# A hybrid decoder trunk on one core: more down-projection fetches and weight sums moved forward, one block of sums taken out of the up weights' buffers, merge operands without precedence

## The chip, the cores and the metric

The kernel runs on one core of a Trainium2 chip. The metric is device time in microseconds (us). The engines are TensorE (PE, with its weight loads as PEld), VectorE (DVE), ScalarE (ACT), GpSimd (POOL) and SyncE (SP), which issues all DMAs here, one after the other in a fixed order.

## The reference

One layer of a decoder trunk on x of 1024 tokens by 1024 features, float32. The two mixers, which the change does not touch, are left out here.

```python
h = rms_norm(x, norm_mix_pre);  proj = h @ w_in          # columns for mixers A, B and two gates
y_a = gdn_branch(...) @ w_out_a                          # gated DeltaNet, 4 heads
y_b = gla_branch(...) @ w_out_b                          # gated linear attention, 4 heads
merged = sigmoid(gate_a) * y_a + sigmoid(gate_b) * y_b
x = x + rms_norm(merged @ w_o, norm_mix_post)            # called x1 below
h = rms_norm(x, norm_mlp_pre)
u = square(relu(h @ w_mlp_up))                           # 1024 x 4096
x = x + rms_norm(u @ w_mlp_down, norm_mlp_post)
```

## The kernel before

**Arithmetic.** Every float32 operand is cut into a high part (rounded to the PE's fp32r type by a cast on ACT) and a low part (the rest, a subtraction on DVE, in fp32r as well). A 128x512 output over 128 of the contraction takes three matmuls (high by high, high by low, low by high). `split` and `hilo` do the cutting; in the listings a weight `w` becomes `wh` and `wl`, and a `big` or `R` tile holds both parts of a block. A "product" is a 128x128x4 block of weights against a 512x512 block of activations: four steps of three, twelve matmuls (L68).

**Stages.** Input projection and mixers; the merge stage, whose `load_o` fetches the mixers' outputs slice by slice and cuts each into `hi` and `lo`; the output projection W_o, in a pool `op`; the up projection, in a pool `ml`; the down projection, in a pool `dn`. The MLP's two multiplications are done as seven products of sums of blocks instead of eight products of blocks (Strassen-Winograd): tokens and features are halved, and P1 to P7 are the seven products. A "unit" n is one pair of 128-wide column blocks of w_mlp_up (columns n and n + 16 blocks), so there are 16 units (NU). Units 0 to 7 (NE = 8) have their P1 and P2 computed ahead, in the `op` stage, and do five products in the up stage (`early`); units 8 to 15 do seven.

**The `op` stage.** For token half u = 0, then 1, W_o is multiplied in, and each of the half's four 128-token tiles goes through this chain: x is loaded into `xt` (L1194, tag "ss", two buffers); x1 is made in it on DVE (L175) and stored to DRAM, `d_x1` (L1196, `d_x` in the profile); ACT squares it (L178), POOL makes the reciprocal root (L172, L186), and DVE writes the normalised tile into `m` (L175). `turn(u, i)` then transposes tile i of half u by eight PE transposes (L72) into two PSUM banks and makes the operand blocks from them: X["11"], X["21"] and R["11"], R["21"] for u = 0; for u = 1 R["22"], and from sums with the first half's blocks T1, T2, X["22"], X["21"], by way of X["12"] (T3 and T4 follow from X["22"] and X["21"]). The four turns of u = 0 stand in the loop of the second half's W_o. Those of u = 1 stand in the loop that computes P1 and P2 of units 0 to 7, two units at a time: P1 of both, then P2 of both, so the loop has 32 products, here numbered from 0. `TURNS[1]` = (2, 4, 6, 8) puts the four turns, called turn 0 to 3 below, after the matmuls of products 2, 4, 6 and 8 of that numbering as the program is written; where the scheduler then puts them is shown further down. Of the 32 products the text below deals with the first sixteen. For each product 256 KB of weights are loaded (L1210) into a tile `raw` of the pool `wraw` (tag "w", four buffers) and cut into `wh` and `wl` (pool `wsp`, three buffers); the result is evacuated to `e` and stored to `d_p` or `d_u[0]` (L1228).

**Weights of the up stage.** `prep(n)` loads a unit's two column blocks (1 MB, as two `wu` DMAs, L1108) into a `ztile` (tag "wu", four buffers) and makes the sums for its products on DVE: three operations, and a fourth for units below 8. The four X blocks are such ztiles too, so unit 0's prep, which stands after the loop, gets the buffer of an X block. In the up stage prep(n + 2) is called in unit n.

**The down stage.** `down_sums(j)` loads three 256 KB blocks of w_mlp_down (`us`, L1304; tag "us", six buffers, which the unit's own sums, `u_sums`, share), makes two sums and stores them to `d_t`. It is called for two j in each of units 8 to 15. The down stage's seven products (in the order P1, P2, P6, P5, P7, P4, P3) read their operands by `fetch(p, j, pool, place)`, a load of 512 KB of activations (`ru`) and one of 512 KB of weights (`rv`, L1250); what it returns, `parts`, cuts both (L1269 on ACT, L166 on DVE) into a `big` tile (four buffers) when called. Each such pair feeds 24 matmuls. In the last unit, four fetches of P1 (j = 0, 2, 4, 6) are issued ahead of that unit's P3 into tiles R11 and R21, whose old contents (the operands of P1 and P2) are then no longer needed; three are cut there too, the fourth at the end of the unit.

**What sets the order.** A list scheduler places every instruction by when its operands and buffers come free in its own model and by the program's order; `tc.high_priority` lets the instructions in its block go ahead of others that are ready. Each engine then runs its list in that fixed order, and SP issues the DMAs in its list one by one: a DMA that has to wait for a buffer or for data holds up all DMAs behind it. Eight semaphores serve the DMAs in rotation.

Of the kernel before, what the change touches and what calls it, by code (L numbers as in the profile page):

```python
# [16 lines left out]
P = 128  # L17
# [116 lines left out]
def kernel(  # L134
# [30 lines left out]
    def tt(out, a, b, op, eng=None):  # L165
        (eng or V).tensor_tensor(out=out, in0=a, in1=b, op=op)  # L166
# [866 lines left out]
    with tc.tile_pool(name="mp", bufs=1, reuse_waits="tile") as mp:  # L1033
        def load_o(src, n, nm):
            hi = mp.tile([P, n, S], F32R, name=nm + "H")
            lo = mp.tile([P, n, S], F32R, name=nm + "L")
            for k in range(n):
                for u in range(2):
                    us = slice(u * 512, u * 512 + 512)
                    raw = mp.tile([P, 512], F32, tag="oraw", name="oraw", bufs=2)  # L1040
                    SP.dma_start(out=raw, in_=src[k, :, us])
                    with tc.high_priority(offset=HP):
                        A.copy(out=hi[:, k, us], in_=raw)
                        tt(lo[:, k, us], raw, hi[:, k, us].bitcast(F32), ALU.subtract)
            return hi, lo
        oaH, oaL = load_o(d_oa, 4, "oa")
        obH, obL = load_o(d_ob, 8, "ob")
        run(gate_groups([int(c) for c in GTAIL.split()]))
        hp.release()
        bot = tc.alloc_tile_pool(name="bot", bufs=4, side="right", reuse_waits="tile")  # L1050

        def big():
            return bot.tile([P, 8, 512], F32R, tag="big", name="big")

        mg_ = [(big(), big()) for _ in range(2)]
        for c in range(4):
            def sl(w):
                return lambda s: [w[:, 2 * s:2 * s + 2, c * 256:c * 256 + 256]]
            ya = gemm_fm(sl(woa), 4, oaH, oaL, banks=[[mbank("r"), mbank("o")], [mbank("l"), mbank("t")]] if c == 0 else None)
            ga = {}  # L1060
            for b in range(2):
                for u in range(2):
                    sg = mp.tile([P, 512], F32, tag="sa", name="sa", bufs=4)
                    SP.dma_start(out=sg, in_=d_sig[c * 2 + b, :, u * 512:u * 512 + 512])
                    with tc.high_priority(offset=HPE):
                        tt(sg, ya[b][u], sg, ALU.mult)
                    ga[b, u] = sg
            yb = gemm_fm(sl(wob), 8, obH, obL)
            for b in range(2):
                for u in range(2):  # L1070
                    us = slice(u * 512, u * 512 + 512)
                    sg = mp.tile([P, 512], F32, tag="sb", name="sb", bufs=2)
                    SP.dma_start(out=sg, in_=d_sig[8 + c * 2 + b, :, us])
                    with tc.high_priority(offset=HPE):
                        tt(sg, yb[b][u], sg, ALU.mult)
                    mg = ga[b, u]
                    with tc.high_priority(offset=HPM):
                        tt(mg, mg, sg, ALU.add)
                    A.copy(out=mg_[u][0][:, c * 2 + b, :], in_=mg)
                    tt(mg_[u][1][:, c * 2 + b, :], mg, mg_[u][0][:, c * 2 + b, :].bitcast(F32), ALU.subtract)  # L1080
# [19 lines left out]
    def ztile():  # L1100
        return z.tile([P, 2 * KT * P], F32, tag="wu", name="wu", bufs=4)
# [22 lines left out]


    with tc.tile_pool(name="op", bufs=1, reuse_waits="tile") as op:
        X = {n: ztile().rearrange("p (k c) -> p k c", c=512) for n in ("12", "11", "21", "22")}
        wpost = row_bc(norm_mix_post[0], D, "wpost", op)
        wpre2 = row_bc(norm_mlp_pre[0], D, "wpre2", op)

# [8 lines left out]
        def turn(u, i):  # L1139
            m = msu[u][i]  # L1140
            il = slice(i * P, i * P + P)
            pv = []
            for g in range(2):
                pt = gbank() if u else mbank("tl"[g])
                for k in range(4):
                    T.transpose(out=pt[:, k * P:(k + 1) * P], in_=m[:, (g * 4 + k) * P:(g * 4 + k + 1) * P],
                                identity=ident)
                pv.append(pt.rearrange("p (k c) -> p k c", c=P))
            if u == 0:
                for g, n in enumerate(("11", "21")):  # L1150
                    A.copy(out=X[n][:, :, il], in_=pv[g])
                    hilo(R[n], k4, il, X[n][:, :, il])
            else:
                x11, x21, x12, x22 = (X[n][:, :, il] for n in ("11", "21", "12", "22"))
                A.copy(out=x12, in_=pv[0])
                tt(x22, pv[1], x12, ALU.subtract)
                hilo(R["22"], k4, il, pv[1])
                tt(x12, x12, x11, ALU.subtract)
                tt(x11, x22, x11, ALU.add)
                hilo(T2, k4, il, x11)  # L1160
                hilo(T1, k4, il, x12)
                tt(x21, x21, x11, ALU.subtract)
# [40 lines left out]
        for n in range(0, NE, 2):  # L1203
            pair = range(n, n + 2)
            bank = {}
            for p, k0, blk in (("P1", 0, R["11"]), ("P2", 4, R["21"])):
                for m in pair:
                    raw = wraw.tile([P, 2, 256], F32, tag="w", name="w").rearrange("p a c -> p (a c)").rearrange(
                        "p (k c) -> p k c", c=P)
                    SP.dma_start(out=raw, in_=wup[:, k0:k0 + 4, m * P:m * P + P])  # L1210
                    hi, lo = split(raw, [P, 4, P], wsp, "w")
                    if p == "P1":
                        bank[m] = mbank("ro"[m % 2])
                    for k in range(4):
                        mm3(bank[m], hi[:, k, :], lo[:, k, :], blk[:, k, :], blk[:, 4 + k, :],
                            p == "P1" and k == 0, k == 3, p == "P2")
                    step = 2 * n + (2 if p == "P2" else 0) + m - n
                    if step in TURNS[1]:
                        turn(1, TURNS[1].index(step))
                    e = op.tile([P, 512], F32, tag="e", name="e", bufs=3)  # L1220
                    with tc.high_priority(offset=HPM):
                        if p == "P1":
                            A.copy(out=e, in_=bank[m])
                        else:
                            act(e, bank[m], AF.Relu)
                    if p == "P2":
                        act(e, e, AF.Square)
                    SP.dma_start(out=d_p[m] if p == "P1" else d_u[0][:, m, :], in_=e)  # L1228
        prep(0)
        T3, T4 = big(), big()  # L1230
        for k in range(0, 4, 2):
            hilo(T3, slice(k, k + 2), slice(0, 512), X["22"][:, k:k + 2, :])
# [42 lines left out]
    with tc.tile_pool(name="ml", bufs=1, reuse_waits="tile") as ml:  # L1275
# [93 lines left out]
        def s_P3(n):  # L1369
            x = un[n]  # L1370
            product(n, "P3", x["C"], False)
            with tc.high_priority(offset=HPM):
                tt(x["c12"], x["C"], x["c12"], ALU.add)
            relu2(x["c12"], x["c12"])
# [48 lines left out]
        for n in range(NU):  # L1423
            if n + 1 < NE:
                again(n + 1)
            if n < NE:
                early(n)
                u_sums(n)
                continue
            s_P6(n)  # L1430
            if n + 2 < NU:
                prep(n + 2)
            s_P5(n)
            s_P7(n)
            if n >= NU // 2:
                down_sums(2 * n - NU)
            if n + 1 < NU:
                s_P1(n + 1)
                s_P4(n)
                s_P2(n + 1)  # L1440
                s_P3(n)
            else:
                if n == NU - 1:

                    r = [hp2.tile([P, 8, 512], F32, tag=t, name="r" + t) for t in ("R11", "R21")]
                    places = [(r[q // 2][:, q % 2 * 4:q % 2 * 4 + 2], r[q // 2][:, q % 2 * 4 + 2:q % 2 * 4 + 4])
                              for q in range(4)]
                    ahead = [fetch("P1", 2 * q, None, places[q]) for q in range(4)]
                    ahead[:3] = [f() for f in ahead[:3]]
                s_P3(n)  # L1450
                s_P4(n)
            if n >= NU // 2:
                down_sums(2 * n - NU + 1)
            u_sums(n)
        ahead[3] = ahead[3]()
    z.release()


    with tc.tile_pool(name="dn", bufs=1, reuse_waits="tile") as dn:
# [4 lines left out]
        def products(p, banks, first, tail=False):  # L1464
            todo = []
            for j in range(0, NU, 2):
                todo.append((j, ahead.pop(0) if ahead else fetch(p, j, dn)()))
                if tail and j == NU - 4:
                    continue
                if tail and j == NU - 2:  # L1470
# [131 lines left out]
```

## Time and profile before

| what | value |
|---|---|
| median of 3 runs | 1677.91 us (1676.59 to 1677.92) |
| the profiled execution | 1680.88 us, of which its span is 1679.2 us |
| granted PE clock, mean | 0.996 |
| PE busy | 1637.6 us, 8398 matmuls |
| DVE, ACT, POOL busy | 1002.1, 785.9, 134.8 us |
| DMA | 255.56 MB, mean 152 GB/s |
| loads `wu` | 32 of 512 KB, 5.7 us each from issue to landing |
| loads `us` | 48 of 256 KB, 4.7 us |

In the views, a row of a timeline begins with the start and the duration in us, then the engine (SPq is SP's queue, where the time of a DMA's issue stands), the line, the operation, the tile written and the tile read, and how many like instructions follow each other; a bracket at the end gives how long the engine had idled before it and what ended that. A row of waits gives who waited, for whom, then the sum of us, the count and the longest. A row of windows gives, for a stretch, its length, each engine's busy time with its instructions, the granted PE clock (PEclk, 1.00 is full), and the share of the core's DMA engines that was busy, which can come out a little over 1.

### The profile page before, as it was taken

How to read it: one execution, taken by the hardware profiler on the slowest of the kernel's cores; microseconds unless marked ns; L12 is line 12 of the kernel's file. 1: busy time of each engine (PE TensorE's matmuls, PEld its weight loads, DVE VectorE, ACT ScalarE, POOL GpSimd, SP SyncE). 2: the span in 40 equal slices, each digit the busy share in tenths (PEclk: the TensorE clock that was granted, in tenths of full speed). 3: DMA queues.
4: the chain of work that ended last, by engine and by line, in shares of the span. 5: the costliest groups of instructions: out<-in, count | busy, mean ns of one | idle time of the engine just before them, and what ended most of it. 6: DMA issues, size and time to landing. Idle time of an engine off the chain costs nothing. (4 is left out here: it accounts for less than half of the span.)

```text
span 1679.2 us, 23073 instructions
## 1 busy us (share of the span) xinstructions
PE 1637.6 (98%) x8398; PEld 1357.6 (81%) x8398; DVE 1002.1 (60%) x1714; ACT 785.9 (47%) x1629; POOL 134.8 (8%) x225
## 2 busy tenths in 40 slices
PE   7999999999999999999999999999999999999998
PEld 6887778878888888888788888778888887888886
DVE  5677555872455548453444545988777655564764
ACT  5556554644544355343421235754555545443442
POOL 3010111111000000011100011200000000000021
PEclk9999999999999999999999999999999999999999
DMA  5222212221222212224633345686588798786764
GB/s 170 56 75 76 86 38 85 76 79 63 88 69 70 63 51 76 76 57 150 212 109 101 110 160 176 224 275 225 197 275 283 243 311 314 257 272 222 244 220 152
DMA packets 186720, 255.56 MB, mean 152 GB/s; under 512 B 23639, under 2 KB 104622, under 8 KB 186606
## 3 DMA queue, kind: packets, MB, share of 16 engines
q1 hardware_dynamic: 186606, 254.09, 46.9%
q8 instruction: 66, 1.08, 0.3%
q14 instruction: 48, 0.39, 0.1%
HBM read 190.05 MB, written 63.98 MB: 151 GB/s over the span
## 5 line engine op out<-in xcount | busy, mean ns | idle before, releaser
L68 PE MATMUL g<-hT,wh 128*128 128x512 f32 (+1 forms) x728 | 289.4, 398 | 3.1 <-ACT sg L178 2.3
L68 PE MATMUL g<-hL,wh 128*128 128x512 f32 (+1 forms) x728 | 283.4, 389 | 0.0
L68 PE MATMUL g<-hT,wl 128*128 128x512 f32 (+1 forms) x728 | 283.1, 389 | 0.0
L166 DVE TENSOR_TENSOR wl<-w,wh 128x512 fp32r<-128x512 f32 x197 | 135.4, 689 | 215.7 <-ACT wh L237 206.6
L237 ACT CAST wh<-w 128x512 fp32r<-128x512 f32 x200 | 123.7, 619 | 211.7 <-PE g L68 202.4
L68 PE MATMUL g<-big 128*128 128x512 f32 x768 | 175.3, 389 | 2.2 <-ACT big L1269 2.2
L68 PEld LDWEIGHTS g<-big 128*128 128x128 f32 x768 | 144.0, 188 | 32.9 <-ACT big L1269 2.6
L68 PEld LDWEIGHTS g<-hT,wh 128*128 128x128 f32 x728 | 137.9, 190 | 27.9 <-ACT sg L178 2.7
L68 PEld LDWEIGHTS g<-hT,wl 128*128 128x128 f32 x728 | 137.8, 189 | 26.9 <-DVE wl L166 0.2
L68 PEld LDWEIGHTS g<-hL,wh 128*128 128x128 f32 x728 | 138.1, 190 | 22.9
L166 DVE TENSOR_TENSOR big<-ru,big 128x1024 fp32r<-128x1024 f32 x52 | 63.7, 1225 | 110.0 <-ACT big L1269 109.6
L1269 ACT CAST big<-ru 128x1024 fp32r<-128x1024 f32 x52 | 54.7, 1053 | 151.2 <-PE g L68 53.1
L68 PE MATMUL g<-wh,hT 128*128 128x256 f32 (+1 forms) x256 | 87.1, 341 | 0.4 <-ACT gk L841 0.4
L68 PE MATMUL g<-wl,hT 128*128 128x256 f32 (+1 forms) x256 | 86.7, 339 | 0.0
L68 PE MATMUL g<-wh,hL 128*128 128x256 f32 (+1 forms) x256 | 86.5, 338 | 0.0
L68 PE MATMUL g<-wh,big 128*128 128x512 f32 x256 | 81.1, 393 | 0.0
L68 PE MATMUL g<-big,wh 128*128 128x512 f32 x256 | 79.1, 389 | 1.4 <-DVE c L166 1.4
L178 ACT ACTIVATE c<-c 128x512 f32<-128x512 f32 x104 | 64.2, 630 | 26.2 <-DVE c L166 24.1
L166 DVE TENSOR_TENSOR big<-rv,big 128x1024 fp32r<-128x1024 f32 x52 | 63.4, 1220 | 0.2
L68 PE MATMUL g<-R,wh 128*128 128x512 f32 x192 | 59.1, 389 | 0.0
L68 PEld LDWEIGHTS g<-big,wh 128*128 128x128 f32 x256 | 48.0, 188 | 11.7 <-DVE c L166 1.8
L68 PEld LDWEIGHTS g<-wh,big 128*128 128x128 f32 x256 | 48.0, 188 | 11.1 <-DVE m L166 1.1
(461 smaller groups left out, 3372.5 us busy)
## 6 DMA issues: line engine op xcount, KB each, us to landing
ru<-d_u SPq DMA_DIRECT2D x52, 512.0 KB, 4.7
w<-in_w_in_dram SPq DMA_DIRECT2D x96, 256.0 KB, 2.7
rv<-in_w_mlp_down_dram SPq DMA_DIRECT2D x36, 512.0 KB, 5.3
wu<-in_w_mlp_up_dram SPq DMA_DIRECT2D x32, 512.0 KB, 5.7
d_u<-c SPq DMA_DIRECT2D x56, 256.0 KB, 2.8
d_u<-us SPq DMA_DIRECT2D x48, 256.0 KB, 3.2
us<-in_w_mlp_down_dram SPq DMA_DIRECT2D x48, 256.0 KB, 4.7
xt<-in_x_dram SPq DMA_DIRECT2D x16, 512.0 KB, 5.1
```

The costliest lines, as they stand in the source:

```text
L68: return self.eng.matmul(out, lhsT, rhs, start=start, stop=stop, skip_group_check=more)
L166: (eng or V).tensor_tensor(out=out, in0=a, in1=b, op=op)
L178: A.activation(out=out, in_=a, func=func, **kw)
L237: A.copy(out=hi, in_=raw)
L1269: A.copy(out=s4[:, i], in_=raw)
```

## The change

Four things are edited.

1. The cast and the subtraction in `load_o` lose their `high_priority`.
2. X["12"] is no longer a ztile. Each of the four turns of u = 1 takes, where it wrote into X["12"], a 128x4x128 tile `x12` from `wraw`, tag "w", the four buffers that the weights of P1 and P2 use. And `prep(0)` is called within the loop, ahead of the evacuation of product 9 (`TURNS[1][-1] + 1`), instead of after it.
3. `down_sums` is called three times in each of units 8 to 12 and once in unit 13, instead of twice in each of units 8 to 15. In a unit one call stands after P7, the others before `u_sums`, as before.
4. Six fetches instead of four are issued ahead for the down stage's P1. The two more (j = 8, 10) go to a new tile R22 of the pool `hp2`, in the place of R["22"], after the last unit's P3. The first three are still cut at once; the others are cut when their turn in the down stage comes (before, the fourth was cut at the end of the last unit).

```diff
@@ load_o
-                    with tc.high_priority(offset=HP):
-                        A.copy(out=hi[:, k, us], in_=raw)
-                        tt(lo[:, k, us], raw, hi[:, k, us].bitcast(F32), ALU.subtract)
+                    A.copy(out=hi[:, k, us], in_=raw)
+                    tt(lo[:, k, us], raw, hi[:, k, us].bitcast(F32), ALU.subtract)
@@ the op stage
-        X = {n: ztile()... for n in ("12", "11", "21", "22")}
+        X = {n: ztile()... for n in ("11", "21", "22")}
...
-                x11, x21, x12, x22 = (X[n][:, :, il] for n in ("11", "21", "12", "22"))
+                x11, x21, x22 = (X[n][:, :, il] for n in ("11", "21", "22"))
+                x12 = wraw.tile([P, 4, P], F32, tag="w", name="x12")
...
                     if step in TURNS[1]:
                         turn(1, TURNS[1].index(step))
+                    if step == TURNS[1][-1] + 1:
+                        prep(0)
                     e = op.tile([P, 512], F32, tag="e", name="e", bufs=3)
...
-        prep(0)
         T3, T4 = big(), big()
@@ the up stage, units 8 to 15
-            if n >= NU // 2:
-                down_sums(2 * n - NU)
+            sums = list(range(3 * (n - NU // 2), min(3 * (n - NU // 2) + 3, NU)))
+            for j in sums[:1]:
+                down_sums(j)
...
-                    ahead[:3] = [f() for f in ahead[:3]]
+                    ahead[:3] = [(lambda v: lambda: v)(f()) for f in ahead[:3]]
                 s_P3(n)
+                if n == NU - 1:
+                    r2 = hp2.tile([P, 8, 512], F32, tag="R22", name="rR22")
+                    ahead += [fetch("P1", 8 + 2 * q, None, (r2[:, 4 * q:4 * q + 2], r2[:, 4 * q + 2:4 * q + 4]))
+                              for q in range(2)]
                 s_P4(n)
-            if n >= NU // 2:
-                down_sums(2 * n - NU + 1)
+            for j in sums[1:]:
+                down_sums(j)
             u_sums(n)
-        ahead[3] = ahead[3]()
@@ the down stage, products
-                todo.append((j, ahead.pop(0) if ahead else fetch(p, j, dn)()))
+                todo.append((j, (ahead.pop(0) if ahead else fetch(p, j, dn))()))
```

How the scheduler's order moves is seen at three places. In these rows a number after a name is that of a buffer; `mr` and `mo` are the two PSUM banks of the products, `g` those of the transposes, `R_9043` and `R_9044` are R["11"] (operand of P1) and R["21"] (of P2); `d_u_93` to `d_u_99` are d_u[0] to d_u[6].

SP's queue in the `op` stage, from the first weights of the P1 and P2 loop on, before:

```order
L1210 DMA w<-in_w_mlp_up_dram 128x4x128 x6
L1196 DMA d_x_89<-xt 128x1024
L1210 DMA w<-in_w_mlp_up_dram 128x4x128
L1228 DMA d_p<-e 128x512
L1194 DMA xt<-in_x_dram 128x1024
L1196 DMA d_x_89<-xt 128x1024
L1228 DMA d_p<-e 128x512
L1210 DMA w<-in_w_mlp_up_dram 128x4x128 x2
L1194 DMA xt<-in_x_dram 128x1024
L1196 DMA d_x_89<-xt 128x1024
L1228 DMA d_u_93<-e 128x512 x2
```

The same place after the change (the stores of `e` are now on line 1230):

```order
L1210 DMA w<-in_w_mlp_up_dram 128x4x128 x3
L1196 DMA d_x_89<-xt 128x1024
L1230 DMA d_p<-e 128x512
L1194 DMA xt<-in_x_dram 128x1024
L1196 DMA d_x_89<-xt 128x1024
L1230 DMA d_p<-e 128x512
L1210 DMA w<-in_w_mlp_up_dram 128x4x128 x2
L1196 DMA d_x_89<-xt 128x1024
L1194 DMA xt<-in_x_dram 128x1024
L1230 DMA d_u_93<-e 128x512
L1210 DMA w<-in_w_mlp_up_dram 128x4x128 x2
L1108 DMA wu<-in_w_mlp_up_dram 128x8x128
```

Three weight loads stand at the head of the list instead of six; the fourth (product 3) stands behind two stores of x1, two of `e` and an `xt` load, and unit 0's `wu` load now stands here, within the loop.

PE at the end of product 2 (the last row of bank `mr`) and the start of product 3, before:

```order
L68 MATMUL mr<-R_9044,wl 128x512
L72 MATMUL g<-ident,m 128x128 x8
L68 MATMUL mo<-R_9044,wh 128x512 x2
L68 MATMUL mo<-R_9044,wl 128x512
L68 MATMUL mo<-R_9044,wh 128x512 x2
```

After the change:

```order
L68 MATMUL mr<-R_9044,wl 128x512
L72 MATMUL g<-ident,m 128x128 x16
L68 MATMUL mo<-R_9044,wh 128x512 x2
L68 MATMUL mr<-R_9043,wh 128x512 x2
L72 MATMUL g<-ident,m 128x128 x2
L68 MATMUL mo<-R_9044,wl 128x512
```

Turn 1 (the second group of eight transposes) stands right behind turn 0, ahead of product 3, and the first two matmuls of product 4 (`mr` with R_9043) and the first two transposes of turn 2 stand in the middle of product 3.

SP at the end of the up stage, where the fetches ahead are issued (`rR` is such a fetch), before:

```order
L1250 DMA rR_12656<-in_w_mlp_down_dram 128x2x512
L1318 DMA d_u_94<-c_12715 128x512
L1304 DMA us<-in_w_mlp_down_dram 128x512 x3
L1318 DMA d_u_96<-us 128x512
L1306 DMA d_t_100<-us 128x512
L1318 DMA d_u_97<-us 128x512
L1308 DMA d_t_101<-us 128x512
L1318 DMA d_u_98<-c_12604 128x512
L1318 DMA d_u_99<-us 128x512
L1462 DMA wpost_12753<-in_norm_mlp_post_dram 128x1024
L1250 DMA ru<-d_u_93 128x1024
L1250 DMA rv<-in_w_mlp_down_dram 128x2x512
```

After the change (line 1251 is what 1250 was, 1319 what 1318 was, 1467 what 1462 was):

```order
L1319 DMA d_u_95<-c_12662 128x512
L1251 DMA rR_12712<-d_u_93 128x1024
L1251 DMA rR_12712<-in_w_mlp_down_dram 128x2x512
L1251 DMA rR_12712<-d_u_93 128x1024
L1251 DMA rR_12712<-in_w_mlp_down_dram 128x2x512
L1319 DMA d_u_96<-us 128x512
L1319 DMA d_u_94<-c_12733 128x512
L1319 DMA d_u_97<-us 128x512
L1319 DMA d_u_98<-c_12627 128x512
L1319 DMA d_u_99<-us 128x512
L1467 DMA wpost_12756<-in_norm_mlp_post_dram 128x1024
L1251 DMA ru<-d_u_93 128x1024
```

The last unit's sums of down weights (`us` loads, `d_t` stores) are gone from here, and the fifth and sixth fetch (`rR_12712`, the new tile R22) stand ahead of the unit's last stores.

More of the change, by code (lines that the diff above doesn't have):

```diff
@@ L1126 @@
     with tc.tile_pool(name="op", bufs=1, reuse_waits="tile") as op:
-        X = {n: ztile().rearrange("p (k c) -> p k c", c=512) for n in ("12", "11", "21", "22")}
+        X = {n: ztile().rearrange("p (k c) -> p k c", c=512) for n in ("11", "21", "22")}
         wpost = row_bc(norm_mix_post[0], D, "wpost", op)
```

## The prediction

> **What bounds the kernel now.** I read the page's busy times first, then who waited for whom on PE, then stretches of time around the lines that the diff touches, then the order of time in them. The page says that TensorE works nearly always and at full clock:
>
> ```profile
> span 1679.2 us, 23073 instructions
> PE 1637.6 (98%) x8398; PEld 1357.6 (81%) x8398; DVE 1002.1 (60%) x1714; ACT 785.9 (47%) x1629; POOL 134.8 (8%) x225
> PEclk9999999999999999999999999999999999999999
> ```
>
> The change takes no matmul away, so all that it can gain is idle time of PE: 1679.2 - 1637.6 = 41.6 us in all, most of it before 800 us, where nothing is moved. The waits in the two places it touches (1048 to 1120, and after 1360), and the busy time of each engine by stretches:
>
> ```profile
> PE mr L68 <- ACT e L178: 2.2, 2, 1.5
> PE g L68 <- DVE c L166: 1.4, 1, 1.4
> PE mo L68 <- ACT e L178: 0.4, 1, 0.4
> PE g L68 <- ACT big L1269: 2.2, 1, 2.2
> ```
>
> ```profile
> core 0: us, PE busy (x) PEld busy (x) DVE busy (x) ACT busy (x) POOL busy (x), PEclk, DMA share, GB/s
> 1048.00:1080.00 32.00, 31.59 (x155) 26.09 (x154) 27.84 (x38) 23.26 (x47) 11.07 (x20) 1.00 0.71 231
> 1080.00:1100.00 20.00, 18.70 (x79) 14.19 (x77) 18.03 (x27) 15.35 (x27) 0.00 (x0) 1.00 0.78 242
> 1100.00:1120.00 20.00, 17.75 (x77) 14.39 (x78) 16.26 (x27) 8.81 (x17) 0.00 (x0) 1.00 0.79 247
> 1120.00:1240.00 120.00, 120.00 (x531) 99.38 (x530) 95.42 (x152) 62.01 (x104) 0.00 (x0) 1.00 0.69 228
> 1260.00:1280.00 20.00, 20.00 (x90) 16.57 (x89) 14.90 (x24) 11.18 (x19) 0.00 (x0) 1.00 0.85 285
> 1380.00:1400.00 20.00, 17.76 (x78) 14.05 (x77) 12.18 (x10) 10.83 (x11) 2.79 (x1) 1.00 1.02 374
> ```
>
> PE idles 0.41 + 1.30 + 2.25 = 4.0 us between 1048 and 1120, 2.2 at 1388, and not at all in the units between. So 6.2 us (0.37%) is nearly the most there is to win, and a step that makes PE wait anywhere counts in full. A matmul starts every 0.226 us (120 / 531), a product of twelve takes 2.72.
>
> **Merge operands.** Without its precedence load_o stands in the same order on ACT, DVE and SP as before: 0. A loss or gain would need another order.
>
> **Six fetches ahead.** The first down product outruns the four that lie ready:
>
> ```profile
> 1379.27 0.45 SPq L1250 DMA_DIRECT2D ru<-d_u  x1
> 1379.77 0.43 SPq L1250 DMA_DIRECT2D rv<-in_w_mlp_down_dram  x1
> 1387.04 1.04 ACT L1269 CAST big<-rv 128x1024 fp32r<-128x1024 f32 x1 [0.33 <-DMA rv<-in_w_mlp_down_dram]
> 1388.13 4.04 PE L68 MATMUL g<-big 128*128 128x512 f32 x15 [2.19 <-ACT big L1269]
> ```
>
> The rv issued at 1379.77 is cast at 1387.04 and PE waits 2.19 us. In the new order this fetch and the next stand in R22, whose loads wait only for the last P3 (it ends near 1363), so they have some 20 us. Each pair feeds 24 matmuls, 5.44 us, so the first fetch that is not ahead (the seventh) is needed 2 x 5.44 us later than the fifth was, at about 1396.7, and no later step of SP is behind it that wasn't. The wait goes, with the slow restarts of two halves of the fetch: -2.8 (at least its 2.2). Late next is nothing.
>
> **Sums of down weights.** Per unit three instead of two in units 8 to 12: five more transfers of 256 KB and two more DVE subtractions. At 0.85 of the DMA engines the unit moves 5.5 MB in its 19.04 us; 6.8 MB would need, in proportion, 0.85 x 26 / 21 = 1.05 of them, and 1.02 is the most a row shows. What overflows is 0.7 us a unit, 3.5 in five units. It is hidden if it falls on the sums, which nobody reads before the down stage, and costs 3.5 if it falls on the weight loads; but the unit after next's weights are fetched a whole unit ahead (19 us). DVE, the queue behind them, has 5 us idle in 20. I take 0, with +3.5 as the other end. A gain is excluded: no PE idle stands there.
>
> **x12 in the weights' buffers, unit 0's weights early.** Here the order moves most: three loads of weights (L1210) ahead instead of six, the second turn's transposes ahead of product 3 (products 0 to 15 are those of P1 and P2 in this stage, turn 0 to 3 the transposes of the second half's tiles). What the loads and the chain take now:
>
> ```profile
> 1034.83 13.97 SPq L1210 DMA_DIRECT2D w<-in_w_mlp_up_dram  x6
> 1051.13 0.34 SPq L1196 DMA_DIRECT2D d_x<-xt  x1
> 1054.92 0.34 SPq L1194 DMA_DIRECT2D xt<-in_x_dram  x1
> DMA to landing us min/median/max: 2.7/3.3/5.1
> ```
>
> ```profile
> 1055.41 1.28 DVE L175 SCALAR_TENSOR_TENSOR xt<-m,rs,xt 128x1024 f32<-128x1024 f32 x1
> 1056.60 0.68 DVE L166 TENSOR_TENSOR wl<-w,wh 128x512 fp32r<-128x512 f32 x1
> 1056.78 1.06 ACT L178 ACTIVATE m<-xt 128x1024 f32<-128x1024 f32 x1 [0.68 <-POOL rs L172]
> 1057.74 1.03 PE L72 MATMUL g<-ident,m 128*128 128x128 f32 x8
> 1057.84 0.60 ACT L237 CAST wh<-w 128x512 fp32r<-128x512 f32 x1
> 1058.02 0.19 POOL L172 TENSOR_SCALAR rs<-rs 128x1 f32<-128x1 f32 x1 [0.33 <-ACT m L178]
> 1058.29 0.54 POOL L186 TENSOR_TENSOR rs<-rs,mhalf 128x1 f32<-128x1 f32 x1
> 1058.53 0.71 PE L68 MATMUL mo<-R,wh 128*128 128x512 f32 x2
> 1058.86 1.28 DVE L175 SCALAR_TENSOR_TENSOR m<-xt,rs,wpre 128x1024 f32<-128x1024 f32 x1 [1.57 <-POOL rs L186]
> ```
>
> With these durations, and 0.4 us for an issue on SP, I walk the new order by hand.
> Product 3's load stood fourth of the six (1042.99); now it is behind a store of x1, a store of e, an xt load that waits until 1054.92, and two more stores: issued at 1056.9, landed at 1060.2 (3.3), at worst 1062.0.
> Turn 0 ends at 1058.53 as now. Turn 1, which now follows it, needs the second tile's m. Its xt is 0.6 us earlier than in the rows (the wl between is gone): done 1056.1, square 1057.3, POOL 1058.5, m at 1059.8. PE waits 1.3, then turns until 1060.6.
> Product 3's cast stands on ACT behind the square of the third tile, whose xt lands near 1059.4: xt done 1061.0, square 1062.2, cast 1062.8. PE waits 2.2. Its next matmuls are two of product 4 and two transposes of turn 2, for which the third m comes at 1064.5, and the split of product 3 is behind that on DVE (1065.15): 2.3 us with 1.1 of work, so 1.2 more. Product 4 ends at 1069.7.
> Product 5's load reuses product 3's buffer: issued 1065.2, landed 1068.5, cast in time (at 5.1 us 1.2 late). Two splits behind the last tile's two long operations on DVE cost 0.2 and 0.5. Turns 2 and 3 end at 1077.3.
> Product 7's load now stands behind the store of product 5's e, which is copied at 1073.2: issued 1073.7, landed 1077.0. ACT has the evacuation of product 6 and two x12 copies before its cast: done 1079.2, a wait of 1.9. Its split is behind the four operations of unit 0's preparation that now stand there (0.6 each): 1080.7, 0.7 more.
> Product 9's load (1080.8, landed 1084.1) is in time for 1085.5 (0.9 late at 5.1 us). Products 12 and 14 wait 0.5 and 0.2 for evacuations, as product 12 did.
> Unit 0's weights lie ready, so the 1.5 us wait at its start goes, and c22, for which PE waited 1.4, is at 1115.8 just in time.
> The sum is 1.3 + 2.2 + 1.2 + 0.7 + 1.9 + 0.7 + 0.7 = 8.7 us of idle instead of 4.0: +4.7. The lower end: the first three alone, all later ones hidden, 4.7 - 4.0 = +0.7. The upper: loads at 5.1 us, 8.7 + 1.2 + 0.9 + 0.2 - 4.0 = +7.0. I stay with +4.7, as most of its waits hang on ACT's and DVE's order and not on a landing.
>
> **The clock.** A stall can cost more than itself. Earlier in the kernel stands one of the same length:
>
> ```profile
> 806.70 0.52 PE L68 MATMUL g<-hT,wh 128*128 128x512 f32 x1 [2.30 <-ACT sg L178]
> 807.88 0.63 PE L68 MATMUL g<-hT,wh 128*128 128x512 f32 x1
> 808.31 0.63 PE L68 MATMUL g<-hL,wh 128*128 128x512 f32 x1
> 810.68 0.39 PE L68 MATMUL g<-hL,wh 128*128 128x512 f32 x1
> 807.00:810.40 3.40, 3.40 (x9) 2.63 (x8) 1.28 (x2) 1.37 (x3) 1.02 (x2) 0.51 0.75 240
> ```
>
> After 2.30 us of idle the granted clock is 0.51 for 3.4 us and a matmul starts every 0.43 instead of 0.226: eight of them, 1.6 us. After the 2.19 at 1388 it stayed 1.00. The new order has two thin stretches, 1057.7 to 1065.2 and 1075.9 to 1080.7, mostly transposes and waits. Each may bring such a drop, 0 to 1.6 us; part of a drop falls into waits that are there anyway. I take half of one, +0.8, ends 0 and +3.2.
> The Trainium skill (TensorE: Matmul & The Clock Gate, What's actually happening) lets the clock halve after an idle window of about 3.4 us. By that rule alone no wait above would do it and the sum would be 0.8 lower; the trace disagrees, since 2.30 us were enough. The same page (Part 4: PE-mode transpose) says that transposes don't count as busy time; then the stretch from 1057.7 to 1062.8 is one idle of 5.1 us, a drop is certain and the sum is 0.8 to 2.4 higher. No run here shows that part.
>
> **Sum.** 0 - 2.8 + 0 + 4.7 + 0.8 = +2.7 us against the profiled execution (1680.88, span 1679.2), so 1683.6 for such a one. It was 3.0 above the median of the runs, 1677.91; the same step from the median gives 1680.6. About 0.2%, 3.4 us, is what a measurement of this kernel can tell from no change, so the line is at 1681.3.
>
> **Rivals.**
> Faster: the lateness of products 3 to 9 doesn't reach PE, because a load takes 3.3 us and a product 2.72, so that little lead is needed; the early weights of unit 0 then clear all 4.0 us. -4.0 - 2.8 = -6.8, 1671.1. For it speaks that DVE, ACT and the loads all keep up now; against it that product 3's cast stands behind a square whose data land at 1059.4, after the 1058.53 at which PE wants it. It decides if that cast begins before 1058.5.
> Milder: the first three waits come and the rest is absorbed: +0.7 - 2.8 = -2.1, 1675.8.
> Slower by the clock and long loads: both drops in full and loads at 5.1 us: 7.0 - 2.8 + 3.2 = +7.4, 1685.3. For it speaks the row at 806.70 and the DMA share of 0.71 that the early preparation adds 1 MB to.
> Slower by the sums: the overflow reaches the weights, +3.5 more, 1684.1. It decides if the DMA share in units 9 to 12 is 1.0 and PE waits for a split behind us.
>
> **How the numbers follow.** The chain as walked, with 0 to 1.6 for the clock, 0.50 (1678 to 1682.5; 0.30 of it within the bound, 0.20 above); milder 0.11 (no change); clock and long loads 0.17 and sums 0.10 (slower); faster rival 0.12. So faster 0.12, no change 0.41, slower 0.47; the forecast itself stands just inside the bound. The range runs from 1675.0, below the milder case, to 1686.0, above the two slow ones; the faster rival and a tail are left out. The likeliest case's own range is 1678 to 1682.5.
>
> **What would show it.** Right: no wait of PE for big near 1385 to 1395; PE waiting at turn 1 for m, at product 3 for wh and at product 7 for wh and wl, 8 to 9 us idle between 1048 and 1120; no PE wait at unit 0's P6; DMA share near 1.0 in units 8 to 12 with PE at 20.00 of 20. Wrong: idle under 5 us between 1048 and 1120 (the faster rivals), PE below full between 1240 and 1340 (the sums), a granted clock of 0.5 at either thin stretch (the clock), or any change at 806.

## The result, and the profile after

The change makes the kernel slower: 1689.61 us median of 6 runs (1686.54 to 1691.87) against 1678.06 (1676.59 to 1680.63), a ratio of 1.0065, 95% interval 1.0052 to 1.0079. The forecast was 1680.6, range 1675.0 to 1686.0. The profiled execution took 1691.87. Its page, first lines:

```profile
span 1690.1 us, 23074 instructions
PE 1642.9 (97%) x8398; PEld 1360.7 (81%) x8398; DVE 1001.2 (59%) x1714; ACT 783.7 (46%) x1629; POOL 135.0 (8%) x225
```

The same 8398 matmuls keep PE busy 5.3 us longer, so some of them ran at a lower clock, and PE idles 47.2 us instead of 41.6. Where, the windows say (length, then busy time of PE, PEld, DVE, ACT and POOL, PEclk, DMA share, GB/s), first of the changed kernel, then (the last two rows) 1280 to 1340 of the kernel before:

```profile
1048.00:1080.00 32.00, 26.83 (x121) 20.23 (x119) 26.45 (x36) 20.46 (x40) 9.76 (x18) 0.95 0.73 238
1080.00:1100.00 20.00, 19.61 (x86) 16.25 (x87) 17.87 (x27) 16.89 (x29) 0.00 (x0) 1.00 0.78 237
1100.00:1120.00 20.00, 17.11 (x70) 13.57 (x69) 13.48 (x22) 6.94 (x12) 0.00 (x0) 0.93 0.74 238
...
1280.00:1300.00 20.00, 18.69 (x83) 15.16 (x82) 14.12 (x23) 8.72 (x16) 0.00 (x0) 1.00 0.86 287
1300.00:1340.00 40.00, 37.92 (x160) 30.78 (x159) 28.25 (x45) 18.74 (x34) 0.00 (x0) 0.96 0.91 303
1380.00:1400.00 20.00, 20.00 (x90) 16.57 (x89) 12.19 (x13) 10.38 (x13) 2.79 (x1) 1.00 0.91 323
...
1280.00:1300.00 20.00, 20.00 (x90) 16.57 (x89) 14.53 (x24) 10.47 (x19) 0.00 (x0) 1.00 0.83 285
1300.00:1340.00 40.00, 40.00 (x178) 33.10 (x177) 26.57 (x43) 21.85 (x38) 0.00 (x0) 1.00 0.69 239
```

Between 1048 and 1120 PE idles 5.17 + 0.39 + 2.89 = 8.45 us (before: 4.0); between 1280 and 1340 it idles 1.31 + 2.08 = 3.4 where it had not idled at all; from 1380 on the idle 2.2 is gone. For whom PE waited, in 1048 to 1120 and in 1280 to 1345 (sum, count, longest):

```profile
PE mo L68 <- ACT wh L237: 3.1, 2, 1.9
PE g L68 <- DVE c L166: 2.9, 1, 2.9
PE g L72 <- DVE m L175: 1.0, 2, 0.8
PE mo L68 <- DVE wl L166: 1.0, 1, 1.0
PE mr L68 <- ACT wh L237: 0.3, 1, 0.3
...
PE mr L68 <- ACT c L1344: 2.1, 1, 2.1
PE mo L68 <- ACT c L1344: 1.3, 1, 1.3
```

Three stretches at about half clock (PEclk) come with them:

```profile
1064.00:1066.10 2.10, 2.10 (x6) 1.66 (x7) 2.10 (x4) 0.57 (x1) 0.00 (x0) 0.54 0.73 232
1118.00:1124.00 6.00, 6.00 (x15) 4.65 (x16) 3.42 (x7) 1.88 (x3) 0.00 (x0) 0.50 0.39 131
1311.50:1315.20 3.70, 3.70 (x11) 2.89 (x10) 3.67 (x7) 0.85 (x2) 0.00 (x0) 0.54 0.90 318
```

At 0.226 us each, 6, 15 and 11 matmuls cost 1.4, 3.4 and 2.5 us; here they took 2.1, 6.0 and 3.7, so the clock cost 0.7 + 2.6 + 1.2 = 4.5 us.

If the matmuls are numbered in the order in which they run, and the same number is looked up in both traces, the difference grows like this: -1.4 us up to 1055 of the time before, +5.0 from there to 1110, +4.4 to 1125, 0 to 1260, +5.7 to 1320, +0.2 to 1380, -2.8 to 1395, 0 to the end: +11.0. The -1.4 belongs to no edit: no order changed up to there. It is +0.8 up to 800 and -2.2 at 806, where PE stopped for 2.30 us in the profiled execution of before, with half clock behind it, and for 1.67 without in that of the changed kernel. In the other traces this stop is anything from under 1.0 to 2.2 us, so a change at 806, which the prediction named as a sign of being wrong, is a sign of nothing. The profiled execution of before was itself 3.0 above its median.

Two places in the trace show the mechanisms. First, unit 0's third product (bank `g`):

```profile
1108.11 1.21 SPq L1108 DMA_DIRECT2D wu<-in_w_mlp_up_dram  x2
1109.38 1.55 SPq L1297 DMA_DIRECT2D p<-d_p  x1
...
1115.83 0.69 DVE L166 TENSOR_TENSOR c<-mr,p 128x512 f32<-128x512 f32 x1 [4.54 <-DMA p<-d_p]
1116.43 0.68 DVE L166 TENSOR_TENSOR wl<-ss,wh 128x512 fp32r<-128x512 f32 x1
1117.03 0.68 DVE L166 TENSOR_TENSOR c<-g,c 128x512 f32<-128x512 f32 x1
...
1117.77 1.22 PE L68 MATMUL g<-big,wh 128*128 128x512 f32 x2 [2.89 <-DVE c L166]
```

On SP, the load of unit 0's stored P1 (`p`) stands behind a load of weights for unit 4, which waits until 1108 for a buffer. DVE idles 4.54 us for `p`, and frees the bank only two operations later.

Second, units 8 and 9, where PE waits for an evacuation on ACT:

```profile
1279.13 0.69 DVE L166 TENSOR_TENSOR us<-us 128x512 f32<-128x512 f32 x1 [4.89 <-DMA us<-in_w_mlp_down_dram]
...
1285.28 0.69 DVE L166 TENSOR_TENSOR us<-us 128x512 f32<-128x512 f32 x1
1285.88 0.68 DVE L166 TENSOR_TENSOR c<-g,c 128x512 f32<-128x512 f32 x1
...
1286.60 1.29 ACT L178 ACTIVATE c<-c 128x512 f32<-128x512 f32 x2
1287.80 0.60 ACT L1286 CAST wh<-wu 128x512 fp32r<-128x512 f32 x1
1288.31 0.58 ACT L1344 COPY c<-mo 128x512 f32<-128x512 f32 x1
...
1288.94 0.73 PE L68 MATMUL mo<-big,wh 128*128 128x512 f32 x2 [1.31 <-ACT c L1344]
```

A subtraction of `down_sums` (`us<-us`) waits 4.89 us at the head of DVE's queue for its load. From 1279.13 DVE works off its queue without a pause; `c` comes out late at 1285.88, ACT squares it, and only then copies the bank that PE wants.

### The profile page after: what moved, and what is told of

The parts are those of the page before. It is cut to its first block, busy times and chain, and to the rows that moved or that the text cites. A ratio compares the mean times of both kernels' runs of the same rounds, so it can differ in the third digit from the quotient of the medians.

```text
span 1690.1 us, 23074 instructions
## 1 busy us (share of the span) xinstructions
PE 1642.9 (97%) x8398; PEld 1360.7 (81%) x8398; DVE 1001.2 (59%) x1714; ACT 783.7 (46%) x1629; POOL 135.0 (8%) x225
```

## The experiments

Each kernel has 4 to 12 runs, in four groups with runs of the kernel before in each; those have medians of 1677.53 (sums undone, x12 undone, six fetches, GpSimd for the subtractions), 1678.28 (seventh buffer, x12 in its own buffer, unit 0's products on another queue, and that x12 with two sums), 1678.57 (stores on GpSimd, copies, and the two combinations at the end) and 1678.65 (small copies, one sum in 16 units). A ratio is to the kernel before in the same group. The changed kernel was not timed again in them: what a run is "less" or "more" than it is taken from 1689.61 by the medians, and such a difference is uncertain by 2 to 3 us.

**The sums undone.**

```diff
-            sums = list(range(3 * (n - NU // 2), min(3 * (n - NU // 2) + 3, NU)))
+            sums = [2 * n - NU, 2 * n - NU + 1]
```

> The changed kernel with two sums of down weights per unit in units 8 to 15 again, everything else as changed. Theory (DVE's queue): in units 8 to 10 a subtraction of the sums stands on DVE ahead of a result that ACT must square before it can copy a bank that PE wants; it waits for its load, so PE waits (2.08 us at 1310, 1.31 at 1289) and runs at half clock for 8 matmuls. Then both waits and the slow stretch go here: 5.0 to 5.7 us less than the changed kernel's 1689.6, about 1684, PE 20.00 of 20 from 1280 to 1340. Rival (the waits come from the order that x12 moved, not from the sums): they stay, 1689.

1684.11 us, ratio 1.0039 (1.0027 to 1.0052): 5.5 less than the changed kernel. Both waits and the slow stretch behind them are gone from its trace (PE waits for `c` of L1344 for 0.2 us in all), so three sums a unit made them, although their results are not read before the down stage.

**x12 and unit 0's preparation undone.** X["12"] is a ztile again, `prep(0)` stands after the loop.

> The changed kernel with x12 in a fourth block of the up weights' buffers and unit 0's preparation after the loop, as before; sums and fetches as changed. Theory: the chain of products (net 5.0 us against before) and the wait for unit 0's stored P1 with the half clock after it (net 4.4) go: 9.4 less, about 1680, and the waits at units 8 to 10 stay. Rival (the waits of the sums hang on the shift of everything by 8 us): those go too, about 1675.

1680.65, ratio 1.0018 (1.0009 to 1.0027): 9.0 less. Its trace still has waits at units 8 to 10 (3.0 us), so these don't hang on the shift.

**Six fetches alone**, added to the kernel before.

> The kernel before with six fetches ahead, and nothing else of the change. Theory: the 2.2 us wait at the down stage's third pair goes with its slow restarts: 2.8 less than before, 1675.2; PE 20.00 of 20 there. Rival (with the last unit's sums still in the queue the two fetches come later, behind them): the wait stays in part, 1676 to 1678.

1674.49, ratio 0.9986 (0.9977 to 0.9995): 3.0 less. Its windows have PE full:

```profile
1380.00:1400.00 20.00, 20.00 (x90) 16.58 (x89) 9.85 (x9) 9.49 (x9) 2.79 (x1) 1.00 1.01 376
```

The three parts add up: 5.5 + 9.0 - 3.0 = 11.5, and the change made 1689.61 - 1678.06 = 11.55. So close a sum is luck: by the ratios the parts are 4.4, 7.9 and -2.3, together 9.9 of 10.9, each uncertain by 1.5 to 3 us. In the traces they are 5.7, 9.4 and -2.8.

**x12 in a buffer of its own.** Moving `prep(0)` alone back behind the loop leaves the order of every engine as it is, so the scheduler would have put it there anyway as soon as a ztile is free; what is left to test is x12's place:

```diff
-                x12 = wraw.tile([P, 4, P], F32, tag="w", name="x12")
+                x12 = op.tile([P, 512], F32, tag="jk", name="jk", bufs=1).rearrange("p (k c) -> p k c", c=P)
```

> The changed kernel with x12 in a buffer of its own (one, that of a tile no longer in use) instead of the weights' four; unit 0's weights stay as early as in the change. Theory (x12 takes the buffers that the loads of P1's and P2's weights need): the waits of the chain of products go and the 1.5 us at unit 0's start stays away; unit 0's wait for its stored P1 may stay: 5 to 6.5 less, 1683 to 1684.6. Rival (the 1 MB and the four operations of unit 0's preparation in the middle of the chain make the waits): less than 1.5 is gained, 1688 to 1690.

1683.38, ratio 1.0033 (1.0021 to 1.0045): 6.2 less than the changed kernel. PE's waits between 1048 and 1120:

```profile
PE g L68 <- DVE c L166: 1.6, 1, 1.6
PE mo L68 <- ACT e L178: 1.4, 1, 1.4
PE mr L68 <- ACT e L178: 0.3, 1, 0.3
```

No wait for `wh`, `wl` or `m` is left. The place in the weights' ring made them, not the early preparation, which is still there. At unit 0 PE waits 1.6 us for its sum on DVE, without half clock behind it.

**Unit 0's stored products from another queue.**

```diff
-            SP.dma_start(out=x["p1"], in_=d_p[n])
-            SP.dma_start(out=x["c11"], in_=d_u[0][:, n, :])
+            (SP if n else G).dma_start(out=x["p1"], in_=d_p[n])
+            (SP if n else G).dma_start(out=x["c11"], in_=d_u[0][:, n, :])
```

> The changed kernel with unit 0's two loads of stored products issued from GpSimd's queue instead of SP's. Theory (they stand on SP behind the weights of unit 4, which wait for a buffer until 1108): they land some 3 us earlier, unit 0's wait of 2.9 us and the 14 matmuls at half clock behind it go, 3 to 5.9 less: 1683.7 to 1686.6. Rival (the data land late because the DMA engines are busy): wait within 1 us of 2.9, 1688 to 1690.

1685.7 (1682.92 to 1693.21), ratio 1.0054 (1.0037 to 1.0070): 3.9 less by the medians, but the interval overlaps that of the changed kernel, so the time alone shows little. The trace shows more. The two loads go out at 1070 and 1076 instead of behind 1108, and DVE makes the sum at once when its bank is ready:

```profile
1111.69 0.69 DVE L166 TENSOR_TENSOR c<-mr,p 128x512 f32<-128x512 f32 x1
```

PE waits for nothing at unit 0, so the wait and the half clock behind it were SP's order. Matched by matmul number, that place (1110 to 1125) is 6.1 us shorter than in the changed kernel; 2.7 us of it were lost again behind the turns, where this execution had half clock for longer and a second time at 1080.

**Why the sums' loads are late.** Six kernels. GpSimd for the subtractions (`eng=G` in `down_sums`):

> The changed kernel with the two subtractions of each sum of down weights on GpSimd instead of DVE, the same loads and stores. Theory (DVE's queue): with the same DMA traffic the waits at 1289 and 1310 and the slow clock go, 5.0 to 5.7 less, about 1684. Rival (the DMAs overflow and the weights themselves land late): PE still waits there, 1688 to 1690. Third (GpSimd slows DVE or comes late itself): slower than 1690.

1698.6, ratio 1.0130 (1.0116 to 1.0144): slower than the change. A subtraction takes 1.4 us there instead of 0.69, SP waits with the stores for it, and the weights' loads behind those stores come late: PE waited 5.96 and 4.41 us for `c`. The place of the sums in DVE's order is gone, but a new wait has taken over; it does not tell the theories apart.

A seventh buffer (`bufs=7` for "us", the room from two unused pads):

> The changed kernel with seven instead of six buffers for the loaded blocks of down weights and the unit's own sums (room from two unused pads); every engine's order is the same but for a few rows of DVE and SP. Theory (the ring of buffers is full with three sums a unit, so each load is issued late and DVE stands behind it): the waits at units 8 to 10 shrink to under 1 us in all, 3 to 5.5 less than the changed kernel's 1689.6: 1684 to 1686.6. Rival (the DMA engines are full and every landing is late): no change, 1688 to 1691.

1692.89, ratio 1.0091 (1.0078 to 1.0104): not faster. DVE's wait for the loads stays, 19.8 us against the changed kernel's 19.3 below. A full ring is not the cause; the theory as written falls.

Stores from GpSimd's queue (`G.dma_start` for the two stores of `down_sums`):

> The changed kernel with the stores of the sums of down weights issued from GpSimd's queue instead of SP's; the same transfers. What is open is why DVE finds the loads late (19.3 us of waiting in units 7 to 10). Theory (a round trip: on SP the next sum's loads stand behind the last sum's stores, which wait for DVE, which waits for loads): without the stores SP issues the loads early, DVE's waits fall below 8 us and PE's waits go: 4 to 5.7 less than 1689.6, 1684 to 1685.6. Rival (the DMA engines are full): 1688 to 1690.

1702.12, ratio 1.0131 (1.0110 to 1.0151). The theory of a round trip between SP and DVE gets no support here: with the stores off SP, DVE still waits 17.2 us for loads between 1248 and 1318. Since the orders of SP and DVE changed with it, it is not excluded either.

Copies that nobody reads, beside two sums a unit:

```diff
             u_sums(n)
+            if NE <= n < 13:
+                for q in range(5):
+                    SP.dma_start(out=d_c[q], in_=d_u[q % 3][:, n - 1, :])
```

> Two sums a unit again (1684.1), and in each of units 8 to 12 five copies of 256 KB from DRAM to DRAM that nobody reads: as many transfers as the third sum has, on SP, but nothing that DVE works on. Theory (the round trip between SP and DVE makes the waits): within 1.5 of 1684.1. Rival (more transfers alone make every landing late): 3 to 6 more, 1687 to 1690, with PE waits between 1270 and 1340.

1692.76, ratio 1.0085 (1.0068 to 1.0102): 8.7 more than without the copies (7.7 by the ratios), and more than either case allowed. Transfers alone are enough to make PE wait. But it is not quite the same wait: DVE waits 11.3 us for the sums' loads there and 6.8 for the up weights (`wu`), for which it never waits in the changed kernel's stretch. The same with `[:, 0:8]`, so 4 KB each:

> As copies (two sums a unit, five copies a unit in units 8 to 12), but each copy moves 4 KB instead of 256 KB. Theory (the bytes: three sums a unit ask for some 350 GB/s, more than the 300 that the changed kernel reached there): the waits of copies go, 1684 to 1685.5 like sums_back. Rival (the number of transfers: SP's queue and its eight semaphores, where each transfer waits for the eighth before it): 1688 to 1692 like copies.

1685.5, ratio 1.0044 (1.0030 to 1.0057): within 1.4 of the kernel without copies. So what the copies cost is their bytes, not their number. The window 1248 to 1318, columns as above, and DVE's waits for the loads there, of the changed kernel:

```profile
1248.00:1318.00 70.00, 66.61 (x285) 54.18 (x284) 49.42 (x80) 33.26 (x59) 0.00 (x0) 0.98 0.90 300
...
DVE us L166 <- DMA us<-in_w_mlp_down_dram: 19.3, 10, 4.9
```

The same of sums_back (two sums a unit):

```profile
1248.00:1318.00 70.00, 70.00 (x311) 57.95 (x310) 50.45 (x80) 38.59 (x67) 0.00 (x0) 1.00 0.85 286
...
DVE us L166 <- DMA us<-in_w_mlp_down_dram: 3.4, 4, 1.2
```

In copies:

```profile
1248.00:1318.00 70.00, 67.50 (x298) 55.56 (x297) 42.62 (x69) 34.75 (x61) 0.00 (x0) 1.00 0.88 293
```

In copies_small:

```profile
1248.00:1318.00 70.00, 69.45 (x307) 57.19 (x306) 47.96 (x78) 36.55 (x64) 0.00 (x0) 1.00 0.86 290
...
DVE us L166 <- DMA us<-in_w_mlp_down_dram: 13.4, 5, 3.5
```

The core moves 286 to 300 GB/s in all four. The loads are no slower for it, though. From issue to landing (the last number, a median) they take as long in the changed kernel (first row) as in sums_back (second):

```profile
us<-in_w_mlp_down_dram SPq DMA_DIRECT2D x27, 256.0 KB, 4.5
...
us<-in_w_mlp_down_dram SPq DMA_DIRECT2D x23, 256.0 KB, 4.8
```

They are issued late. Of the four loads in the next view, DVE waited 4.89 us for the second, which went out only at 1273.78, half a microsecond before DVE wanted it, and landed 5.3 us later. SP had stood at stores that wait for DVE's results; at the stores of the sums (L1307, L1309) that made 24.0 us in this stretch, against 10.6 in sums_back:

```profile
1272.60 0.35 SPq L1319 DMA_DIRECT2D d_u<-us  x1
1273.01 2.81 SPq L1305 DMA_DIRECT2D us<-in_w_mlp_down_dram  x4
...
SPq L1307 <- DVE us L166: 15.2, 9, 3.0
SPq L1309 <- DVE us L166: 8.8, 8, 3.2
```

So DVE waits for loads that SP issues late, and SP is late because it waits for DVE. The record doesn't settle what starts this: taking the stores off SP did not end it, and 256 KB copies bring on waits without a third sum, while the DMA engines are busy for 0.88 to 0.90 of the time, less than the 1.02 they reached at 1380 before. Nor is lateness on DVE the whole of it: in copies_small DVE waits 13.4 us for loads and PE only 0.55. It costs where, as at 1279.13, a result that PE's bank hangs on stands behind the subtraction.

One sum in each of the 16 units (`down_sums(n)` also in units 0 to 7):

> The changed kernel with one sum in each of the 16 units. Theory (bytes): units 8 to 15 have room; units 0 to 7 moved 219 GB/s and get 1.3 MB more in about 15 us each, so some 305 GB/s, just at what was reached: PE waits of 0 to 2 us in all, 1684 to 1686. Rival (any sum on DVE ahead of an evacuation makes PE wait for its load): 8 units with waits of 0.5 us or more, over 1688.

1687.74, ratio 1.0051 (1.0039 to 1.0064). In its trace units 8 to 13 run without a wait of PE, units 0 to 7 have two of 0.4 us for `c`, and the 2.9 at unit 0's start are still there; that execution took 1685.0, as expected. The median is 1.7 above the expected range, and with an interval that touches both sums_back's and the change's this one settles little.

**Toward a faster version.** x12 in its own buffer and two sums a unit:

> The changed kernel with x12 in a buffer of its own and two sums a unit again: what is left of the change is six fetches ahead, unit 0's early weights and the merge operands. Theory: the 3.0 of the fetches, and the 1.5 us wait at unit 0's start is gone; 1673 if unit 0's wait for its stored P1 is no longer than before (1.4), 1677 if it is followed by half clock as in the changed kernel. Rival (chain as in the changed kernel): 1679.

1675.05, ratio 0.9984 (0.9976 to 0.9993): as good as six fetches alone. Unit 0's early weights take away the wait of 1.5 us there, and the whole is no faster for it. Matched by matmul number, the profiled execution is 1.7 us shorter than that of six fetches alone between 1048 and 1110 and 1.5 longer at 806, where no edit reaches; the runs, with intervals of about 1.5 us either way, can't show such a gain. With unit 0's stored products on GpSimd's queue besides:

> The kernel of own_sums_back (1675.05) with unit 0's two loads of stored products on GpSimd's queue. The one wait of over 0.6 us that is left there, 1.4 us for those loads, goes: 1.4 less, 1673.6. Rival (with early weights the place is no longer short of time, or DVE is late itself): 1675.

1678.29, ratio 0.9996 (0.9987 to 1.0005): a miss. PE's wait of 1.4 us for `c` is still there, although `p` lies ready: DVE comes to that sum only at 1108.92, as its queue stood 1.1 us for `wu` up to 1105.78 (the second half of the rival). And the two loads go out at 1067 and 1069, among 512 KB of unit 0's weights and four weight loads of the chain; these took 7.7 us to land instead of 5.2, and PE waits there too:

```profile
1077.52 0.62 ACT L237 CAST wh<-w 128x512 fp32r<-128x512 f32 x1 [1.96 <-DMA w<-in_w_mlp_up_dram]
...
1078.69 0.80 PE L68 MATMUL mo<-R,wh 128*128 128x512 f32 x1 [2.67 <-ACT e L178]
```

Six fetches and that queue, with x12 as before:

> The kernel of ahead_only (1674.5) with unit 0's two loads of stored products on GpSimd's queue: its wait of 1.9 us for them goes, 1.4 to 1.9 less, 1672.6 to 1673.1; x12 and the order before are as in the kernel before. Rival (the 1.5 us wait of unit 0's first product just ahead grows instead): 1674.5.

1675.2, ratio 0.9976 (0.9965 to 0.9987). The wait for the two loads is gone from its trace, but the median, expected at 1672.6 to 1673.1, is no lower than that of the six fetches alone. Against the runs of the kernel before beside it, 1678.57, it is 3.4 less, and 3.0 for the six fetches alone: both beat both kernels, and the intervals overlap.

## Why the prediction was wrong, point by point

**Six fetches: right.** -2.8 forecast; -2.8 in the trace, -3.0 alone.

**Merge operands: as far as seen, right.** Every engine's list is the same with and without the precedence, so there is nothing to time.

**Sums of down weights: the step that failed.** The prediction worked out that three sums a unit ask for more than the DMA engines give, then took 0, because the overflow falls on sums "which nobody reads before the down stage", with 3.5 as the other end. The lateness did fall on the sums. The step that failed is that nobody would feel it there: their subtractions stand in DVE's queue ahead of results that ACT must square before it frees a bank. That cost 3.4 us of idle, 1.2 of half clock and the slow first matmuls after each stop, 5.7 in the trace and 5.5 in the runs. That DVE had 5 us idle in 20 said nothing about it, since it was the order, not the load, that mattered. Nor did the DMA engines overflow as reckoned: 0.7 us a unit (0.6 by its own figures) was worked out with 1.02 of them, but they were busy for 0.90 of the stretch, at 300 GB/s, and the loads were late because they were issued late. What starts that is open.

**x12 and unit 0's weights: the right sum for half wrong reasons.** 8.7 us of idle forecast, 8.45 measured. Turn 1 waited 0.8 (forecast 1.3), product 3 1.9 (2.2) with 0.3 at the next product, product 7 1.2 and 1.0 (1.9 and 0.7); the 1.2 at product 3's split was 0 to 0.2. These are 5.6 us together, less than walked. The rest, 2.9, is the wait that the prediction cleared, so that 8.45 met 8.7 is luck: it had c22 "just in time" at 1115.8, and at 1115.8 only `p` had landed. Queue and load were the same as in the wait of 1.4 before.

**The clock: too small.** 0.8 taken, 3.2 at most, and in the thin stretches only. In this stage it was 0.7 + 2.6 = 3.3, most of it after the wait at unit 0 that was not forecast. Half of one drop was too little for the thin stretches as well: of the nine traces with this chain the first had one in all nine, the second in five (not in the changed kernel's). And each stop has a slow restart (the first matmul behind a stop is followed after 0.34 us instead of 0.23, in the median of 36 stops without half clock), which the prediction counted where a wait went but not where waits came: with it the stage lost 5.0 + 4.4 = 9.4 in the trace, and 9.0 in the runs.

**The rivals.** Slower by the clock and slower by the sums were priced as two cases, 0.17 and 0.10, each added to the walked chain. Nothing made them exclude each other, and both came, which put the time outside the range. The profiled execution was 11.0 slower, 8.3 more than the forecast +2.7: 5.7 from the sums, and 9.4 in the stage of the chain where 4.7 + 0.8 = 5.5 were taken (2.5 of the difference is clock, the rest mostly restarts), less the 1.4 at 806 that belong to no edit. The median missed by 9.0. The lower rivals, 1671.1 and 1675.8, had no part.

## What to carry to other kernels

Work whose result is not needed for long still costs if its operation stands in an in-order queue ahead of one that is needed: price it by what is queued behind it, not by its reader. Before a buffer is shared with a ring of loads, walk the loads that ring carries; here one of four tiles taken for moments cost 6 us, and with a buffer of its own none of those waits was left. In a stage that already moves nearly as much as it was seen to move (286 of 300 GB/s here), an extra transfer is not free, however early it is: five of 256 KB a unit that nobody reads cost 8 us.

## What the runs showed of the hardware

Stops of PE after 800 us with no transposes in the 5 us ahead of them, in all 16 traces: of 26 stops of 1.0 to 1.9 us none was followed by half clock; of 16 stops of 1.95 to 2.65 us six were; of nine stops of 2.7 to 6.0 us all nine, for 6 to 14 matmuls. That is an earlier limit than the 3.4 us of idle that the Trainium skill states (TensorE: Matmul & The Clock Gate, What's actually happening), and for the length of a stop not a sharp one.

Something else is sharp. Between 800 and 1600 us every stretch of half clock in these traces lasts 3.41 us or twice that, and within a trace all of them begin whole multiples of 3.41 us apart. Those of the changed kernel begin 16 and 57 of them apart:

```profile
1062.52:1065.93 3.41, 3.22 (x9) 2.08 (x8) 3.41 (x6) 0.46 (x2) 0.00 (x0) 0.50 0.78 275
1117.13:1123.96 6.83, 6.19 (x15) 4.84 (x16) 4.25 (x8) 1.88 (x3) 0.00 (x0) 0.50 0.35 115
1311.69:1315.11 3.42, 3.42 (x10) 2.65 (x9) 3.38 (x7) 0.76 (x2) 0.00 (x0) 0.50 0.88 314
```

If each trace is cut into ticks of that length (those at half clock left aside), of the ticks without transposes 16 of the 17 that a drop follows had PE busy for 7 to 45% (the other for 61%), and none of some 3500 others for less than 45%. So a stop of about 2 us halves the clock when nearly all of it falls into one tick, and does not when it is spread over two. The ticks lie elsewhere in each trace, so which of the two comes is luck here.

Behind the sixteen transposes of turns 0 and 1, where PE stops for only 1.85 to 2.1 us, all nine traces with that order drop to half clock, six for 3.41 us and three for 6.83; in some few matmuls fall into it, because PE waits there anyway. So the drop was as sure as the prediction read it. But that is no proof of the rule behind it, that a transpose "doesn't count as PE-busy the same way" (the Trainium skill, TensorE: Matmul & The Clock Gate, Part 4: PE-mode transpose). With transposes counted as busy, PE was busy for 32 to 52% of the ticks ahead of these nine drops, and two ticks with no matmuls but transposes (50% busy in the run with seven buffers, 57% in copies) were followed by full clock.
